# A two-layer decoder trunk: both attention mixers built alike, K, V and Q of a head group projected between attention steps, score matmuls of two heads on two row halves in float32r

## The chip, the cores and the metric

One core of a Trainium2 chip runs the whole program. The engines are TensorE (PE, with its weight loads PEld), VectorE (DVE), ScalarE (ACT), GpSimd (POOL) and SyncE (SP), which here only issues DMAs. The metric is the device time of one execution in microseconds (us); a kernel is given by the median of its runs.

## The reference

The input x is 256 tokens of 1024 float32 values. All weights are float32. In short:

```python
for layer in range(2):
    h = h + 0.5 * swiglu(rmsnorm(h, ffn1_norm[layer]), w_gate, w_up, w_down)   # 1024 -> 2816 -> 1024
    hn = rmsnorm(h, mix_norm[layer])
    if layer == 0:
        h = h + mixer_a(hn, a_w_qkv, a_w_o, pos)        # q, k, v from hn
    else:
        h = h + mixer_b(hn, b_w_q, b_w_o, *shared, pos)  # q from hn, k and v shared
    h = h + 0.5 * swiglu(rmsnorm(h, ffn2_norm[layer]), ...)
    if layer == 0:
        shared = shared_kv(h, kv_norm, kv_w, pos)        # k, v from rmsnorm(h, kv_norm)
return rmsnorm(h, final_norm)
```

There are 16 heads of 64 dimensions; the first 16 of q and k are rotated. Mixer A mixes three dilated causal windows by their softmax denominators, which for 256 tokens equals one softmax in which a key counts as often as it stands in the three windows. Mixer B's blocks are 256 long, so it is causal attention over 256 tokens.

## The kernel before

**Arithmetic.** Every large product is done in float32r with two parts: `parts_of` and `pieces_of` make hi (ACT, rounded to float32r) and lo = value - hi (DVE). A product is hi.hi + hi.lo + lo.hi. Weights come by SP's DMA queue in units of up to 1 MB (`unit`, four raw buffers), are split into `wh` and `wl` tiles of 128 x 1024 (eight buffers each), and go to PE.

**Layout.** The stream hT is kept with features on partitions (8 blocks of 128 x 256 tokens). In the FFN the weights are the stationary operand: a step `product_t` for one block of 128 outputs runs eight matmuls of 512 columns (L193: wh against hi and lo of x side by side) and then eight of 256 (L195: wl against hi). `ffn_blocks` does gate and then up for each of 22 blocks of the hidden layer, with `close` (join, norm row, silu, product; the product with the norm row for up is on POOL, L328) between. `down_t` holds the weights of two output blocks, 22 k-blocks each, and runs one output after the other in runs of 8, 8 and 6.

**Mixers.** In the projections the tokens are stationary and weights move (`product`, L183, L185, L187). Mixer A projects q and k of four heads together (512 columns) and v (256), turns q and k by rotation and transposes, and attends to one group while the next is projected (`weave` takes steps from both by declared costs). The K/V stage between the layers projects all of K and V for mixer B into constants kTb and vb; mixer B then projects q alone, in two halves.

**Attention** (`attend`). For a head: scores in plain float32, 64 rows of PE (L491: one matmul of 128 columns for the first 128 queries, one of 256 for the second), mask, scale and row minimum in one DVE operation (L493), exp with a row sum on ACT (L496), reciprocal on DVE (L498), p times it on ACT (L500), three transposes on PE (L511), split into hi and lo (L92, L94), and four matmuls with v (L528 to L531), of 512, 256, 2 x 128 and 2 x 128 columns. Scores are issued three heads ahead (AHEAD) of the transposes, the values one head behind (LATE). The output projection is `out_t` (L419 to L421).

**Buffers and order.** [...] A scheduler orders each engine's instructions from the order of the source and the buffers that come free; each engine then runs its own list in that order.

Of the kernel before, what the change touches and what calls it, by code (L numbers as in the profile page):

```python
# [28 lines left out]
AHEAD = 3  # L29
LATE = 1  # L30
EXTRA = 1
HURRY = 0.5
FILL_B = 10.0
# [33 lines left out]
def trunk(ctx: ExitStack, tc: tile.TileContext, a: dict, out: bass.AP):  # L67
# [121 lines left out]
    def product_t(ac, ws, xs, first, last):  # L189


        for i, ((wh, wl), x) in enumerate(zip(ws, xs)):
            nc.tensor.matmul(ac, wh, flat(x), start=first and i == 0, stop=False)  # L193
        for i, ((wh, wl), x) in enumerate(zip(ws, xs)):
            nc.tensor.matmul(ac[:, :S], wl, x[:, 0, :], start=False, stop=last and i == len(ws) - 1)  # L195


    def gain(k, gi, name):
        x = xp.tile([P, 2, S], F32R, tag=f"x{k}", name=f"x_{name}_{k}")
        g = gT[:, gi * KD + k:gi * KD + k + 1]  # L200
        parts_of(x[:, 0, :], x[:, 1, :], hT[:, k, :], g)
        return x

    class Norm:
# [41 lines left out]
        def xs(self):  # L246

            return [[tuple(x[:, i, t * P:(t + 1) * P] for i in range(2)) for x in self.x] for t in range(NT)]
# [39 lines left out]
    def down_t(name, w, blocks, norm):  # L288

        for p in range(KD // 2):  # L290
            ws = []
            for k0 in range(0, KF, KD):
                k = min(KD, KF - k0)
                ws += unit(f"{name}_{p}_{k0}", k, S, [(None, rows(w, k0, k, p * S, S))])
            for b in range(2):
                d = 2 * p + b
                ac = acc(f"dn_{name}_{d}")
                cut = [tuple(w[:, b * P:(b + 1) * P] for w in pair) for pair in ws]
                for k0 in range(0, KF, KD):
                    k1 = min(k0 + KD, KF)  # L300
                    product_t(ac, cut[k0:k1], blocks[k0:k1], k0 == 0, k1 == KF)
# [11 lines left out]
    def ffn_blocks(name, wg, wu, norm, first=None):  # L313
# [3 lines left out]
        def times(n, f, w):  # L317
            ac = acc(f"{name}_{n}{f}")
            cols = slice(f % 2 * P, (f % 2 + 1) * P)
            product_t(ac, [(wh[:, cols], wl[:, cols]) for wh, wl in w], norm.x, True, True)  # L320
            return ac
# [21 lines left out]
        for f in range(0, KF, 2):  # L343
# [5 lines left out]
            if f == 0:  # L349
                acs = [[acc(f"{name}_{n}{i}") for n in "gu"] for i in range(2)]  # L350
                for k, pair in enumerate(ws):
                    for i in range(2):
                        for ac, (wh, wl) in zip(acs[i], pair):
                            cols = slice(i * P, (i + 1) * P)
                            product_t(ac, [(wh[:, cols], wl[:, cols])], norm.x[k:k + 1], k == 0, k == KD - 1)
# [9 lines left out]
            wg2, wu2 = zip(*ws)  # L365
# [7 lines left out]
    def ffn(name, layer, which, norm, after, first=None):  # L373
        wg, wu, wd = (a[f"ffn{which}_w_{n}"][layer] for n in ("gate", "up", "down"))
        blocks = ffn_blocks(name, wg, wu, norm, first)
# [5 lines left out]
    def down_last(name, w, nk, blocks, h, weight, part, after, tail=4):  # L381
# [17 lines left out]
        for t in range(NT):  # L399
            for i, (c, o, n) in enumerate(segs[t]):  # L400
                for k, ws in held:
                    product(accs[t][i:i + 1], *blocks[t][k], cols(t, ws)[i:i + 1], False, k == nk - 1)
                hc = h[t][:, c, o:o + n]
# [41 lines left out]
    def rotate(v, t, name):  # L445
# [4 lines left out]
        ta = sp.tile([P, n, ROT], F32, tag="rota", name=f"ra_{name}")  # L450
        tb = sp.tile([P, n, ROT], F32, tag="rotb", name=f"rb_{name}")
# [5 lines left out]
    def turned(src, t, r, name):  # L457

        s = atile([P, 8, DH], name=f"rt_{name}")
        nc.scalar.activation(s.rearrange("p a b -> p (a b)"), src, AF.Copy, scale=r)  # L460
        rotate(s, t, name)
        return s.rearrange("p a b -> p (a b)")

    def transposed(s, dsts, t, name):

        n = s.shape[1] // P
        tr = trt(f"qt_{name}")
        for k in range(n):
            nc.tensor.transpose(tr[:, k * P:(k + 1) * P], s[:, k * P:(k + 1) * P], ident)
        for i, dst in enumerate(dsts):  # L470
            nc.vector.tensor_copy(dst[:, :, t, :],
                                  tr[:, 2 * i * P:(2 * i + 2) * P].rearrange("p (k n) -> p k n", n=P))

    def attend(groups, operands, mask, name, blocks):
# [3 lines left out]
        heads = [(g, j) for g in groups for j in range(HG)]  # L478
        sms = {}

        def scores(g, j):
            qT, kT, _ = operands(g)
            b, p0 = j // 2, (j % 2) * DH
            kh = kT[p0:p0 + DH, b].rearrange("p t n -> p (t n)")
            ps = trt(f"s_{name}{g}_{j}")
            sm = sms[g, j] = atile([P, 3 * P], name=f"sm_{name}{g}_{j}")
            nm = sp.tile([P, NT], F32, tag="nm", name=f"nm_{name}{g}_{j}")
            ls = sp.tile([P, NT], F32, tag="ls", name=f"ls_{name}{g}_{j}")
            segs = [slice(t * P, t * P + (t + 1) * P) for t in range(NT)]
            for t, seg in enumerate(segs):  # L490
                nc.tensor.matmul(ps[:, seg], qT[p0:p0 + DH, b, t, :], kh[:, :(t + 1) * P], start=True, stop=True)  # L491
            for t, seg in enumerate(segs):
                nc.vector.tensor_tensor_reduce(sm[:, seg], ps[:, seg], mask[:, seg], scale=-SCALE, scalar=3e38,  # L493
                                               op0=ALU.add, op1=ALU.min, accum_out=nm[:, t:t + 1])
            for t, seg in enumerate(segs):
                nc.scalar.activation(sm[:, seg], sm[:, seg], AF.Exp, bias=nm[:, t:t + 1], scale=-1.0,  # L496
                                     accum_out=ls[:, t:t + 1])
            nc.vector.reciprocal(ls, ls)  # L498
            for t, seg in enumerate(segs):
                nc.scalar.activation(sm[:, seg], sm[:, seg], AF.Copy, scale=ls[:, t:t + 1])  # L500

        for i in range(AHEAD):
            scores(*heads[i])
            yield 0.65
        pTs, ss = {}, {}
        for n in range(len(heads) + LATE):
            if n < len(heads):
                g, j = heads[n]
                tr = trt(f"pt_{name}{g}_{j}")[:, :3 * P]
                for i in range(3):  # L510
                    nc.tensor.transpose(tr[:, i * P:(i + 1) * P], sms[g, j][:, i * P:(i + 1) * P], ident)  # L511
                pT = pTs[n] = pp.tile([P, 2, 3 * P], F32R, tag="pT", name=f"pT_{name}{g}_{j}")
                parts_of(pT[:, 0], pT[:, 1], tr)
                yield 0.35
            if n + AHEAD < len(heads):
                while operands(heads[n + AHEAD][0]) is None:
                    yield None
                scores(*heads[n + AHEAD])
                yield 0.65
            if n < LATE:  # L520
                continue
            g, j = heads[n - LATE]
            pT = pTs[n - LATE]
            po = acc(f"po_{name}{g}_{j}")
            late = po.rearrange("p (i n) -> p i n", i=2)[:, :, P:]
            pair = slice(j // 2 * P, (j // 2 + 1) * P)
            (h0, l0), (h1, l1) = [[v[:, i, pair] for i in range(2)] for v in operands(g)[2]]
            nc.tensor.matmul(po, h0, pT[:, :, :2 * P], start=True, stop=False)  # L528
            nc.tensor.matmul(po[:, :S], l0, pT[:, 0, :2 * P], start=False, stop=False)
            nc.tensor.matmul(late, h1, pT[:, :, 2 * P:], start=False, stop=False)  # L530
            nc.tensor.matmul(late, l1, pT[:, :, 2 * P:], start=False, stop=True)  # L531
            yield 0.55
            if j % 2 == 0:
                ss[g, j // 2] = etile(f"o_{name}{g}_{j}")
            s = ss[g, j // 2]
            own = slice(j % 2 * DH, (j % 2 + 1) * DH)
            nc.scalar.activation(s[own], po[own, S:], AF.Copy)
            nc.vector.tensor_add(s[own], po[own, :S], s[own])
            if j % 2:
                x = atile([P, 2, S], F32R, name=f"oT_{name}{g}{j // 2}")  # L540
                parts_of(x[:, 0], x[:, 1], s)
                blocks.append(x)
                if len(blocks) == KD:
                    table(AF.Silu, x[:, 0, 0:1].bitcast(F32))

    ATT = HG * 1.55

    def project(ac, pieces, xs, k0):

        for t in range(NT):  # L550
            for k, ps in enumerate(pieces):
                product([ac[t]], *xs[t][k0 + k], [ps], k0 + k == 0, k0 + k == KD - 1)
                yield 3 * ac[t].shape[1] / 2400

    def mixer_a(norm, after):
        xs = norm.xs()
        w, wo = a["a_w_qkv"][0], a["a_w_o"][0]
        blocks = []
        n = HG * DH
        qTs, kTs, vss = {}, {}, {}  # L560
# [200 lines left out]
```

## Time and profile before

| | |
|---|---|
| median of 3 runs | 1017.9 us (1016.5 to 1018.32) |
| profiled execution | 1016.7 us, span 1014.9 us |
| PE busy | 1001.2 us, 99% of the span |
| DVE, ACT, POOL busy | 706.7, 601.8, 150.7 us |
| DMA | 176.03 MB, mean 173 GB/s |
| PE clock granted | 0.999 of full speed |

The page is one execution seen by the profiler; the 1.8 us between its span and its time lie around the program. The stages follow each other on PE with hardly a gap: first FFN to 196 us, mixer A to 322, second FFN to 508, K/V stage to 554, third FFN to 739, mixer B to 819, last FFN to the end. PE's matmuls overlap in a pipeline, so "busy" sums are larger than the time that matmuls take from each other; distances between starts tell that.

### The profile page before, as it was taken

To read this page: it belongs to the slowest core of one execution; us is meant where nothing else is said; L and a number is where in the kernel's file an instruction comes from. 1 tells how busy PE (TensorE), PEld (TensorE's weight loads), DVE (VectorE), ACT (ScalarE), POOL (GpSimd) and SP (SyncE) were. 2 spreads that over 40 slices of the span, in tenths; PEclk is the share of its full clock that TensorE was granted. 3 is DMA by queue.
4 is the path that set the end of the run, shared out by engine and by line. 5 is a ranking of instruction groups with operands and counts; after the bars stand their busy time and mean duration, and the time that the engine had idled before them with its cause. 6 is when DMAs were issued, how large, how long until landed. Compare 5 with 4: busy or idle time off the path is not lost.

```text
span 1014.9 us, 15264 instructions
## 1 busy us (share of the span) xinstructions
PE 1001.2 (99%) x5739; PEld 864.5 (85%) x5739; DVE 706.7 (70%) x1284; ACT 601.8 (59%) x1128; POOL 150.7 (15%) x147
## 2 busy tenths in 40 slices
PE   8999999999999999999999999999999999999997
PEld 6888888888889888888888888888877888888786
DVE  7977765667767777766666777766578777777542
ACT  7756654567776565554555566555459966665531
POOL 3221111100002212211100121210100042112000
PEclk9999999999999999999999999999999999999999
DMA  9875455743334655655475555654552246555511
GB/s 310 260 255 167 160 197 183 228 151 121 126 122 128 205 166 189 195 178 185 171 245 166 191 183 166 193 196 159 200 208 69 84 141 204 168 169 208 187 60 42
DMA packets 152154, 176.03 MB, mean 173 GB/s; under 512 B 3472, under 2 KB 139920, under 8 KB 152080
## 3 DMA queue, kind: packets, MB, share of 16 engines
q1 hardware_dynamic: 151648, 174.50, 52.1%
q8 instruction: 45, 0.74, 0.3%
q10 hardware_dynamic: 432, 0.55, 0.2%
q14 instruction: 29, 0.24, 0.1%
HBM read 173.99 MB, written 1.05 MB: 172 GB/s over the span
## 4 chain that ended last, share of the span: by engine, by line
PE 87%; DVE 5%; POOL 3%; ACT 2%; issue 2%; DMA 0%; POOLq 0%; ACTq 0%; DVEq 0%
PE f_g L193 13%; PE f_u L193 13%; PE dn_f L193 11%; PE f_g L195 7%; PE f_u L195 7%; PE dn_f L195 6%; PE dn_f_d L185 2%; PE dn_f_d L183 2%; PE dn_f_d L187 2%; POOL j_f_u L328 2%; PE qk L183 2%; PE qk L187 1%; PE kv L183 1%; PE qk L185 1%; PE kv L187 1%
## 5 line engine op out<-in xcount | busy, mean ns | idle before, releaser
L193 PE MATMUL f_u<-x_n,wh_f_u 128*128 128x512 f32 x688 | 179.5, 393 | 0.9 <-DVE j_f_g L310 0.9
L193 PE MATMUL f_g<-x_n,wh_f_g 128*128 128x512 f32 x688 | 179.7, 393 | 0.0
L328 POOL TENSOR_TENSOR j_f_u<-j_f_u,r_n 128x256 f32<-128x256 f32 x88 | 98.1, 1116 | 419.7 <-DVE j_f_u L310 358.7
L193 PEld LDWEIGHTS f_u<-x_n,wh_f_u 128*128 128x128 f32 x688 | 124.0, 189 | 23.9 <-DVE j_f_g L310 1.1
L193 PEld LDWEIGHTS f_g<-x_n,wh_f_g 128*128 128x128 f32 x688 | 124.0, 189 | 22.6
L193 PE MATMUL dn_f<-act_f,wh_f 128*128 128x512 f32 x528 | 134.1, 393 | 0.8 <-DVE act_f L94 0.7
L92 ACT ACTIVATE act_f<-j_f_g 128x256 fp32r<-128x256 f32 x88 | 36.7, 418 | 129.2 <-DVE j_f_g L329 129.0
L155 DVE TENSOR_TENSOR wl_f_g<-raw_f_g,wh_f_g 128x1024 fp32r<-128x1024 f32 x86 | 106.4, 1240 | 5.7 <-ACT wh_f_g L154 5.6
L193 PEld LDWEIGHTS dn_f<-act_f,wh_f 128*128 128x128 f32 x528 | 94.6, 189 | 18.4 <-DVE act_f L94 2.0
L155 DVE TENSOR_TENSOR wl_f_u<-raw_f_u,wh_f_u 128x1024 fp32r<-128x1024 f32 x86 | 105.1, 1223 | 7.3 <-ACT wh_f_u L154 7.3
L195 PE MATMUL f_g<-x_n,wl_f_g 128*128 128x256 f32 x688 | 102.9, 282 | 0.0
L195 PE MATMUL f_u<-x_n,wl_f_u 128*128 128x256 f32 x688 | 102.7, 282 | 0.0
L195 PEld LDWEIGHTS f_u<-x_n,wl_f_u 128*128 128x128 f32 x688 | 96.4, 190 | 6.7 <-DVE wl_f_u L155 0.4
L195 PEld LDWEIGHTS f_g<-x_n,wl_f_g 128*128 128x128 f32 x688 | 96.4, 190 | 6.3
L154 ACT ACTIVATE wh_f_g<-raw_f_g 128x1024 fp32r<-128x1024 f32 x86 | 89.5, 1048 | 9.8 <-PE f_g L193 3.8
L225 POOL TENSOR_TENSOR ss_n<-ss_n,sq_n 128x256 f32<-128x256 f32 x42 | 41.6, 991 | 361.0 <-issue 185.1
L154 ACT ACTIVATE wh_f<-raw_f 128x1024 fp32r<-128x1024 f32 x72 | 68.6, 981 | 42.0 <-issue 24.1
L154 ACT ACTIVATE wh_f_u<-raw_f_u 128x1024 fp32r<-128x1024 f32 x86 | 86.8, 1049 | 8.4 <-PE f_g L193 6.5
L155 DVE TENSOR_TENSOR wl_f<-raw_f,wh_f 128x1024 fp32r<-128x1024 f32 x72 | 79.9, 1130 | 16.3 <-PE dn_f L195 13.4
L329 DVE TENSOR_TENSOR j_f_g<-j_f_g,j_f_u 128x256 f32<-128x256 f32 x88 | 37.5, 429 | 61.3 <-POOL j_f_u L328 60.0
L195 PEld LDWEIGHTS dn_f<-act_f,wl_f 128*128 128x128 f32 x528 | 72.8, 190 | 5.6
L195 PE MATMUL dn_f<-act_f,wl_f 128*128 128x256 f32 x528 | 74.6, 282 | 0.0
(197 smaller groups left out, 1739.1 us busy)
## 6 DMA issues: line engine op xcount, KB each, us to landing
raw_f_g<-in_ffn_w_gate_dram SPq DMA_DIRECT2D x43, 1024.0 KB, 5.2
raw_f_u<-in_ffn_w_up_dram SPq DMA_DIRECT2D x43, 1024.0 KB, 5.2
raw_f<-in_ffn_w_down_dram SPq DMA_DIRECT2D x24, 1024.0 KB, 5.2
raw_f_d<-in_ffn_w_down_dram SPq DMA_DIRECT2D x11, 1024.0 KB, 4.9
raw_f<-in_ffn_w_down_dram SPq DMA_DIRECT2D x12, 768.0 KB, 4.5
raw_qk<-in_a_w_qkv_dram SPq DMA_DIRECT2D x16, 512.0 KB, 5.5
raw_kv<-in_kv_w_dram SPq DMA_DIRECT2D x8, 1024.0 KB, 6.2
raw_v<-in_a_w_qkv_dram SPq DMA_DIRECT2D x4, 1024.0 KB, 5.2
```

The source lines that it names most:

```text
L92: nc.scalar.activation(hi, src, AF.Copy, scale=scale)
L154: nc.scalar.activation(wh, r, AF.Copy)
L155: nc.vector.tensor_sub(wl, r, wh.bitcast(F32))
L183: nc.tensor.matmul(ac, xh, wh, start=first, stop=False)
L185: nc.tensor.matmul(ac, xh, wl, start=False, stop=False)
L187: nc.tensor.matmul(ac, xl, wh, start=False, stop=last)
L193: nc.tensor.matmul(ac, wh, flat(x), start=first and i == 0, stop=False)
L195: nc.tensor.matmul(ac[:, :S], wl, x[:, 0, :], start=False, stop=last and i == len(ws) - 1)
L225: nc.gpsimd.tensor_tensor(self.ss, self.ss, sq, op=ALU.add)
L328: nc.gpsimd.tensor_tensor(u, u, norm.row, op=ALU.mult)
L329: nc.vector.tensor_mul(g, g, u)
```

## The change

- **One mixer function for both layers.** `mixer` takes two normed streams (for K and V, and for Q) and is called twice. For each group of four heads it projects k and v together (512 columns), then q (256 columns). All projections of a group but the first 50 steps are woven between attention steps. For mixer B the K/V stream is a second set of x tiles (`kx`), made from hT beside the third FFN; the K/V stage, kTb and vb are gone.
- **Scores by pairs of heads in float32r.** q and k are split into hi and lo (`qk` tiles), and the scores of two heads, which lie on partitions 0-63 and 64-127, are issued alternately: hi.hi, hi.lo, lo.hi for each head and each half of the queries, 12 matmuls for a pair, six of 128 columns and six of 256. Scores run one pair ahead of the transposes.
- **p scaled on GpSimd**, 64 operations `tensor_scalar` in place of 64 on ACT.
- **Values**: v is kept as hi and lo side by side (128 stationary columns for one head), and moves p's hi and lo as 256, 256, 128 and 128 columns; the two halves of the result are added.
- **FFN runs of 16**: gate and up of a block together, 16 matmuls of 512 columns and then 16 of 256; in the down stage two outputs together, 16, 16 and 12, reading the weights unit by unit. Joining comes after both.

The three constants AHEAD, LATE, HURRY and the like go; START = 50 comes. Core of the diff:

```diff
-    def product_t(ac, ws, xs, first, last):
+    def products_t(acs, wss, xs, first, last):
+        for ac, ws in zip(acs, wss):
+            for i, ((wh, wl), x) in enumerate(zip(ws, xs)):
+                nc.tensor.matmul(ac, wh, flat(x), start=first and i == 0, stop=False)
+        for ac, ws in zip(acs, wss):
+            for i, ((wh, wl), x) in enumerate(zip(ws, xs)):
+                nc.tensor.matmul(ac[:, :S], wl, x[:, 0, :], start=False, stop=last and i == len(ws) - 1)
...
     def down_t(name, w, blocks, norm):
         for p in range(KD // 2):
+            acs = [acc(f"dn_{name}_{2 * p + b}") for b in range(2)]
             for k0 in range(0, KF, KD):
                 k = min(KD, KF - k0)
+                ws = unit(f"{name}_{p}_{k0}", k, S, [(None, rows(w, k0, k, p * S, S))])
+                cut = [[tuple(v[:, b * P:(b + 1) * P] for v in pair) for pair in ws] for b in range(2)]
+                products_t(acs, cut, blocks[k0:k0 + k], k0 == 0, k0 + k == KF)
...
             for i in (f, f + 1):
-                gate = times("g", i, wg2)
+                acs = both(i, pair)
                 close_all()
-                done.append((i, gate, times("u", i, wu2)))
+                done.append((i, *acs))
...
+        def scores(p):
+            g, b = divmod(p, HG // 2)
+            (hi, lo), _ = operands(g)
+            ps = [trt(f"s_{name}{p}_{i}") for i in range(2)]
+            for t, seg in enumerate(segs):
+                for n, (q, k) in enumerate(((hi, hi), (hi, lo), (lo, hi))):
+                    for i, own in enumerate(owns):
+                        nc.tensor.matmul(ps[i][:, seg], q[own, b, t, :],
+                                         k[own, 2 + b].rearrange("p t n -> p (t n)")[:, :(t + 1) * P],
+                                         start=n == 0, stop=n == 2)
...
+            nc.vector.reciprocal(flat(ls), flat(ls))
+            for i in range(2):
+                for t, seg in enumerate(segs):
+                    nc.gpsimd.tensor_scalar(sms[p, i][:, seg], sms[p, i][:, seg], ls[:, i, t:t + 1], None, op0=ALU.mult)
...
+        def values(p, pTs):
...
+                for n in range(2):
+                    nc.tensor.matmul(ac, v0, pT[:, n, :S], start=n == 0, stop=False)
+                for n in range(2):
+                    nc.tensor.matmul(ac[:, P:], v1, pT[:, n, S:], start=False, stop=n == 1)
+                nc.scalar.activation(s[own], ac[DH:], AF.Copy)
+                nc.vector.tensor_add(s[own], ac[:DH], s[own])
...
+        for p in range(-1, H // 2):
+            if p + 1 < H // 2:
...
+                scores(p + 1)
+                yield 0.8
+            if p < 0:
                 continue
+            pTs = []
+            for i in range(2):
+                pTs.append(turn(p, i))
+                yield (0.35, 0.5)[i]
+            values(p, pTs)
+            yield 0.9
...
+        def feed():
+            yield from projections(0)
+            for g in range(1, NG):
+                yield from finished(g - 1, projections(g))
+            yield from finished(NG - 1, some(wsteps, 16))
+
+        steps = feed()
+        run(some(steps, START))
+        weave(attend(operands, mask, name, blocks), 20.4, steps, 59.0)
         run(some(wsteps, 4 * EXTRA))
         run(wsteps)
...
-    mixer_a(n1, n2)
+    mixer("a", n1, xs, (w, H * DH), (w, 2 * H * DH), n1, xs, (w, 0), a["a_w_o"][0], masks[:, 0, :], n2)
     ffn("f20", 0, 2, n2, n3)
-    shared_kv(n3)
-    n3.x = [gain(k, 4, "n4") for k in range(KD)]
-    ffn("f11", 1, 1, n3, n5)
-    mixer_b(n5, n6)
+    kx = []
+    ffn("f11", 1, 1, n3, n5, beside=[lambda k=k: kx.append(gain(k, 3, "kx", "kx")) for k in range(KD)])
+    w = a["kv_w"]
+    mixer("b", n3, by_token(kx), (w, 0), (w, H * DH), n5, n5.xs(), (a["b_w_q"][0], 0), a["b_w_o"][0], masks[:, 1, :], n6)
```

More of the change, by code (lines that the diff above doesn't have):

```diff
@@ L202, in gain, with by_token @@
         return x
+    def by_token(xs):
+        return [[tuple(x[:, i, t * P:(t + 1) * P] for i in range(2)) for x in xs] for t in range(NT)]
     class Norm:
@@ L537, in attend @@
[L537 to L553, printed above, removed]
@@ new lines, in finished @@
+        def finished(g, steps):
+            for i, cost in enumerate(steps):
+                yield cost
+                if i == 4:
+                    turn_in(g, 1)
+                    yield 0.45
+                if i == 8:
+                    ready.add(g)
+        wsteps = out_t(f"{name}o", wo, blocks, after)
+        def feed():
[3 more added lines that the diff above has]
+            yield from finished(NG - 1, some(wsteps, 16))
```

302 lines of the change are left out of this document (99 added, 203 removed).

## The prediction

> **What bounds the kernel now.** I read the head of the page, the chain by engine, then the waits of TensorE (PE).
>
> ```profile
> span 1014.9 us, 15264 instructions
> PE 1001.2 (99%) x5739; PEld 864.5 (85%) x5739; DVE 706.7 (70%) x1284; ACT 601.8 (59%) x1128; POOL 150.7 (15%) x147
> PE 87%; DVE 5%; POOL 3%; ACT 2%; issue 2%; DMA 0%; POOLq 0%; ACTq 0%; DVEq 0%
> ...
> PE dn_f L193 <- DVE act_f L94: 0.7, 1, 0.7
> ...
> PE ot_bo L420 <- DVE oT_b L94: 0.6, 1, 0.6
> ...
> PE ot_bo L419 <- ACT oT_b L92: 0.3, 1, 0.3
> PE po_b L528 <- DVE o_b L538: 0.2, 1, 0.2
> ```
>
> PE works in 99% of the span, the chain is 87% PE, and in both mixers together PE waits 1.1 us (last three rows). So the time is PE's stream of matmuls: matmul time taken out is gained, a wait put into it is lost. The "busy" of one matmul is its latency, so I price by distances between starts, from timelines.
>
> ```profile
> 195.96:321.74 125.78, 125.78 (x791) 107.02 (x790) 87.94 (x224) 88.25 (x200) 4.90 (x6) 1.00 0.43 142
> 507.52:553.50 45.98, 45.98 (x214) 38.06 (x213) 29.93 (x53) 24.51 (x32) 2.52 (x2) 1.00 0.62 207
> 738.67:818.73 80.06, 78.92 (x486) 64.83 (x485) 60.19 (x179) 64.24 (x173) 2.53 (x2) 1.00 0.38 131
> ...
> 516.44 0.39 PE L185 MATMUL kv<-wl_kv,x_n 128*128 128x512 f32 x1
> 519.84 0.39 PE L185 MATMUL kv<-wl_kv,x_n 128*128 128x512 f32 x1
> 312.01 0.28 PE L419 MATMUL ot_ao<-oT_a,wh_ao 128*128 128x256 f32 x1
> 318.38 0.28 PE L421 MATMUL ot_ao<-oT_a,wl_ao 128*128 128x256 f32 x1
> 571.01 1.84 PE f_g L193 x8
> 668.78 1.84 PE f_u L193 x8
> ```
>
> The windows (length, then busy time of PE, PEld, DVE, ACT, POOL, then clock, DMA share, GB/s) are mixer A, the K/V stage and mixer B: 125.8 + 46.0 + 80.1 = 251.8 us that the change rebuilds. A matmul of 512 columns costs 3.40 / 15 = 0.227 us (15 starts between the two kv rows), one of 256 columns 6.37 / 53 = 0.120. An FFN step of eight of each costs 97.77 / 35 = 2.793, against 8 x 0.227 + 8 x 0.120 = 2.774: each change between the kinds and back costs 0.02.
>
> **Part 1, scores.**
>
> ```profile
> 755.54 0.40 PE L187 MATMUL bq<-wh_bq,x_n 128*128 128x512 f32 x1
> 755.86 0.93 PE L491 MATMUL s_b<-kTb,bqT 64*128 64x128 f32 x8
> 756.73 0.50 PE L183 MATMUL bq<-wh_bq,x_n 128*128 128x512 f32 x1
> ...
> 768.94 0.39 PE L185 MATMUL bq<-wl_bq,x_n 128*128 128x512 f32 x1
> 769.17 0.40 PE L187 MATMUL bq<-wh_bq,x_n 128*128 128x512 f32 x1
> 769.50 0.92 PE L491 MATMUL s_b<-kTb,bqT 64*128 64x128 f32 x4
> 770.35 0.50 PE L528 MATMUL po_b<-pT_b,bv 128*128 128x512 f32 x1
> 770.69 0.28 PE L529 MATMUL po_b<-pT_b,bv 128*128 128x256 f32 x1
> 770.80 0.28 PE L530 MATMUL po_b<-pT_b,bv 128*128 128x256 f32 x1
> 770.92 0.28 PE L531 MATMUL po_b<-pT_b,bv 128*128 128x256 f32 x1
> 771.04 0.40 PE L183 MATMUL bq<-wh_bq,x_n 128*128 128x512 f32 x1
> ...
> 769.50 0.29 PEld L491 LDWEIGHTS s_b<-kTb,bqT 64*128 64x128 f32 x2 [0.37 <-DVE wl_bo L155]
> 769.50 0.41 PEld L491 LDWEIGHTS s_b<-kTb,bqT 64*128 64x128 f32 x3 [0.37 <-DVE wl_bo L155]
> ```
>
> One head is four float32 passes (x4, two per matmul), 769.50 to 770.35 = 0.85 us; the matmul before it lasts 0.33 and the one behind it 0.34 where 0.23 is usual. Weight loads in the set come 0.41 - 0.29 = 0.12 apart, so a pass of 128 columns is about 0.11 and one of 256 about 0.215 (the float32 rate), 0.65 in all. The rest, 0.10 + 0.20 + 0.11 = 0.41 us, is paid for each visit to the 64-row mode. The x8 row decides this part: two heads, in rows 0-63 and 64-127, took 755.86 to 756.73 = 0.87 us together. The halves overlap fully, weight loads included.
>
> Before: 32 heads x 0.65, less one shared pair (0.65), and 32 visits x 0.41: 33.3 us. After: per pair 12 float32r matmuls that alternate between the halves. With 256 columns one is 0.12. With 128 columns no row shows one; its bounds are 0.06 (half of 0.12) and 0.215 (two float32 passes of 0.11 each, rounded down). I take 0.11, the pace of the weight loads. A pair is 3 x 0.11 + 3 x 0.12 = 0.69. In the changed kernel's instruction order the eight sets of a mixer stand in ten stretches (pairs 5 and 7 are cut in two, and six matmuls of pair 7 stand in unmixed threes: +0.33). Sum: 16 x 0.69 + 20 x 0.41 + 0.7 = 19.9. **Gain 13.4 us.** If float32r halves did not overlap, 16 x 0.69 = 11.0 of it is lost; at 0.215 per 128 columns 16 x 3 x 0.105 = 5.0; at 0.06 there are 2.4 more.
>
> [...]
>
> **Part 2, values.** A head is now 0.23 + 3 x 0.12 = 0.59 us (L528 to L531), then two matmuls of 256 columns and two of 128: 2 x 0.12 + 2 x 0.11 = 0.46. **Gain 32 x 0.13 = 4.1 us.** Per 128-column matmul at 0.06 it is 3.2 more; at 0.215 it is 6.7 less, a loss of 2.6.
>
> **Part 3, projections.** Mixer B's q becomes 192 matmuls of 256 columns (23.0) for 96 of 512 (21.8): **loss 1.2 us**. All others keep their columns: the K/V stage is not saved but moves into mixer B, with its 8 MB of DMA (DMA was 0.62 busy there and is 0.38 in mixer B, so no bound). Transposes keep their number. The p scalings leave ACT; the hi/lo split of q and k comes to ACT and DVE, where copies go. DVE's 87.9 + 29.9 + 60.2 = 178 us stay about that in some 240, so DVE does not become the bound.
>
> **Part 4, FFN.** 80 gate/up steps and 36 down steps merge 8 + 8 into 16 + 16 and spare one change each: **gain 116 x 0.02 = 2.3 us**. The down stage reads its last activation after some 11 us where it was half that, so the 0.7 us behind act_f go: **gain 0.7**. The last two outputs of a down stage now end 0.7 us apart, not 7.7; the next stage reads their x after more than 5 us of other matmuls, which covers two lots of some 2 us on DVE and ACT. I cost that, and gate and up joining together, at nothing; without the cover it is about 2 us at the end of each of three such stages.
>
> **Part 5, new waits.** Before, scores ran three heads ahead; now one pair. The chain from a pair's last score to its first transpose:
>
> ```profile
> L493 DVE CUSTOM_DVE_ANT_0 sm_a<-s_a,masks 128x256 f32<-128x256 f32 x16 | 6.7, 417 | 0.0
> L493 DVE CUSTOM_DVE_ANT_0 sm_a<-s_a,masks 128x128 f32<-128x128 f32 x16 | 4.6, 291 | 10.0 <-PE s_a L491 9.8
> L496 ACT ACTIVATE sm_a<-sm_a,nm_a 128x256 f32<-128x256 f32 x16 | 7.9, 494 | 0.0
> L498 DVE RECIPROCAL ls_a<-ls_a 128x2 f32<-128x2 f32 x16 | 2.6, 162 | 5.2 <-ACT sm_a L496 5.2
> L94 DVE TENSOR_TENSOR pT_a<-pt_a,pT_a 128x384 fp32r<-128x384 f32 x16 | 8.8, 553 | 2.0 <-ACT pT_a L92 2.0
> L722 POOL TENSOR_SCALAR var<-ssq,ssq 128x1 f32<-128x1 f32 x2 | 0.6, 299 | 58.5 <-ACT sq L713 58.5
> ...
> 41.41 1.59 POOL L328 TENSOR_TENSOR j_f_u<-j_f_u,r_n 128x256 f32<-128x256 f32 x1 [4.04 <-DVE j_f_u L310]
> ...
> 53.00 0.73 POOL L328 TENSOR_TENSOR j_f_u<-j_f_u,r_n 128x256 f32<-128x256 f32 x1 [4.21 <-DVE j_f_u L310]
> ...
> 41.19 1.21 DVE L155 TENSOR_TENSOR wl_f_u<-raw_f_u,wh_f_u 128x1024 fp32r<-128x1024 f32 x1
> ```
>
> Four reductions 2 x (0.29 + 0.42) = 1.4, a last exponential 0.5, a reciprocal 0.16, two scalings on POOL, and an estimated 0.1 for each of some eight hand-overs (no row isolates one). A one-input scaling on POOL stands in no row: for 256 columns it lies between 0.30 (a single column) and 0.73 (two inputs, undisturbed); I take 0.45, and 0.35 for 128. Sum 3.7.
>
> In the new order pair 0 has 18 q matmuls, the next scores and three more q behind it: 21 x 0.12 + 0.69 + 0.41 = 3.6, a wait of about 0.2. Pairs 1 to 5 have some 6 to 18 us. Pairs 5, 6 and 7 crowd at the end. Behind pair 6 stand 6 transposes, 5 output matmuls, 4 of values and pair 7's scores in two stretches: 0.7 + 0.6 + 0.5 + 1.8 = 3.6, against 3.7 and 0.55 to 1 for pair 5's parts in the same queues: wait about 0.9. Pair 7's reciprocal stands in DVE's queue behind pair 5's two adds, its own reductions, parts of pairs 5 and 6 and a weight split of 1.21: added up (an estimate), its transposes can start 11 us after pair 6's scores, and PE comes to them after 9.2: wait about 1.8. With 0.3 at the last output and 1.1 for the three score buffers, which transposes share, a mixer waits 0.2 + 0.9 + 1.8 + 0.3 + 1.1 = 4.3 us, both 8.6, against 1.1 now: **loss 7.5 us**. Bounds: nothing (the order as good as today's) and 16 (rival 2).
>
> **Sum.** -13.4 - 4.1 + 1.2 - 2.3 - 0.7 + 7.5 = -11.8. The profiled execution took 1016.7 us (span 1014.9 and 1.8 around it), 1.2 below the median of 1017.9; 1016.7 - 11.8 = 1004.9, about 1006 as a median.
>
> **Rivals.** 1, *the scores do not do what they say*: float32r halves take turns. For it: no row shows float32r in a half. Against: the float32 row of 0.87. Then -11.8 + 11.0: about 1017.
>
> 2, *slower, by the scaling on POOL*. Place: POOL's four scalings per pair, behind which pair p's transposes and, in DVE's queue, the next pair's parts wait. The trace shows the mechanism: POOL's multiplication that met a DVE split (41.19 to 42.40) ended at 43.00 and took 1.59, the one beside an idle DVE took 0.73. At 1.59 or nearly for each, two scalings cost some 2.8 in place of 0.8: 2 us more at pairs 0 and 6, and 4 at pair 7, where both pairs' scalings add up: 8 a mixer, 16 in all, about 1022. It decides from 6 us a mixer on. Against: most pairs have 6 us and more in hand, and few splits stand in the crowded end.
>
> [...]
>
> 3, *128 columns of float32r cost 0.215*. For it: the kernel before pairs columns up to 256 for its values. Against: weight loads 0.12 apart. Then -11.8 + 5.0 + 6.7 (the 4.1 gained becomes 2.6 lost): about 1018.
>
> 4, *few new waits*: 1 us a mixer, about 999.
>
> **How the numbers follow.** The forecast has a chance of 0.64 and, with waits of 2 to 7 us a mixer and 128 columns between 0.06 and 0.13, a range of 1000 to 1011. Rival 1 has 0.07, rival 2 0.13, rival 3 0.09, rival 4 0.07. The range of 999 to 1018 takes in rivals 1 and 3 at their centres and leaves out rival 2 and the outer halves of the others. A measurement of this kernel can tell about 0.2%, 2 us, from no change. Faster by that: forecast, rival 4 and a part of rivals 1 and 3 that falls short, 0.76; same: most of rivals 1 and 3, 0.10; slower: rival 2 and the rest, 0.14.
>
> **What would show it.** After: visits of score sets at about 1.1 us for 12 matmuls (1.8 would be rival 1); p scalings at 0.3 to 0.5 us (1.2 and more is rival 2); 128-column values 0.11 apart (rival 3); runs x16 in the FFN; mixers of some 118 to 121 us each, and PE waits of pt on POOL and po on DVE of 3 to 5 us a mixer. Mixers over 124 us, or PE waits over 9 us in one, make the prediction wrong.

## The result and the profile after

The changed kernel takes 1022.9 us (median, 1020.6 to 1027.4), the kernel before 1017.9 (1016.4 to 1018.3): a ratio of 1.0058, 95% interval 1.0037 to 1.0078. It is slower by 0.6%, where 1.2% faster was forecast. The executions of the kernel before lie in two groups about 1.6 us apart, and its profiled one, 1016.7 us, is of the faster group. The profiled execution of the changed kernel took 1023.3 us. The head of its page and its chain by engine:

```profile
span 1021.5 us, 15730 instructions
...
PE 994.7 (97%) x5899; PEld 871.0 (85%) x5899; DVE 724.6 (71%) x1252; ACT 592.0 (58%) x1092; POOL 178.1 (17%) x211
...
PE 88%; ACT 6%; DVE 3%; POOL 1%; issue 1%; DMA 0%; POOLq 0%; ACTq 0%; DVEq 0%
```

PE's busy time is 6.5 us shorter and the span is 6.6 us longer: PE fell from 99% to 97% of it, and ACT has 6% of the chain where it had 2%. What PE waited for (us in total, times, longest):

```profile
PE pt_a L494 <- POOL sm_a L489: 3.7, 5, 1.2
PE pt_b L494 <- POOL sm_b L489: 3.6, 5, 1.2
PE f_u L191 <- DVE j_f_g L309: 2.3, 4, 0.9
PE po_a L508 <- ACT pT_a L89: 2.2, 1, 2.2
PE po_a L508 <- DVE o_a L512: 1.2, 2, 0.8
```

The names end in a and b for mixers A and B; f_u belongs to the FFN. Both mixers wait alike: transposes for p scaled on GpSimd, values for the copies of their own transposes on ACT and DVE. The stretches of time show where it went. The first and last window are mixers A and B; the others are 3.41 us long and follow each other in pairs. Columns: length, busy time of PE, PEld, DVE, ACT, POOL, then granted clock, DMA share, GB/s.

```profile
194.55:325.72 131.17, 123.15 (x822) 107.65 (x821) 87.22 (x208) 81.69 (x183) 30.97 (x38) 0.97 0.40 128
228.61:232.02 3.41, 1.75 (x16) 1.22 (x13) 2.21 (x15) 2.98 (x14) 1.95 (x3) 1.00 0.85 308
232.02:235.43 3.41, 3.41 (x15) 3.13 (x15) 0.73 (x2) 0.68 (x3) 3.41 (x6) 0.50 0.00 0
307.11:310.53 3.42, 1.43 (x10) 0.80 (x9) 2.11 (x3) 1.92 (x4) 3.35 (x4) 1.00 0.00 0
310.53:313.94 3.41, 3.41 (x18) 3.41 (x18) 1.82 (x4) 1.18 (x3) 0.66 (x1) 0.50 0.82 269
696.89:827.75 130.86, 122.74 (x822) 107.49 (x821) 87.29 (x208) 81.78 (x183) 29.99 (x38) 0.97 0.40 128
```

The mixers take 131.2 + 130.9 = 262.0 us, where mixer A, the K/V stage and mixer B took 251.8. PE idles 8.0 and 8.1 us in them. And twice in each mixer the clock is 0.50 for 3.41 us, right behind a stretch in which PE was busy for only 1.75 or 1.43 us in mixer A, and 1.91 or 1.65 in mixer B. The first of these in PE's timeline:

```profile
229.40 0.28 PE L184 MATMUL q_a<-wh_qa,x_n 128*128 128x256 f32 x1
230.75 0.33 PE L494 MATMUL pt_a<-ident,sm_a 128*128 128x128 f32 x1 [1.08 <-POOL sm_a L489]
231.67 0.44 PE L494 MATMUL pt_a<-ident,sm_a 128*128 128x128 f32 x2 [0.58 <-POOL sm_a L489]
...
233.16 0.42 PE L180 MATMUL q_a<-wh_qa,x_n 128*128 128x256 f32 x1
233.37 0.42 PE L182 MATMUL q_a<-wl_qa,x_n 128*128 128x256 f32 x1
...
235.60 0.28 PE L180 MATMUL q_a<-wh_qa,x_n 128*128 128x256 f32 x1
235.72 0.28 PE L182 MATMUL q_a<-wl_qa,x_n 128*128 128x256 f32 x1
```

Pair 0's transposes wait twice; after that a matmul of 256 columns takes 0.21 us from start to start, until at 235.43 it is 0.12 again. Idle time in the row of PE is not all that a wait costs.

From the distances between PE's starts (as in the prediction), mixer A's 131.2 us are, by estimate: 117.9 of matmuls at their usual distances, 9.9 by which the starts that waited stand further apart (8.0 of it idle time; the rest fits that a matmul of 256 columns is busy for 0.28 us, while the next usually starts after 0.12), and 3.4 for half of the two stretches at half clock. Mixer B has 117.6, 10.0 and 3.2. The prediction had 117.2 (251.8 less the old waits of 1.1 and less 13.4 and 4.1, plus 1.2, halved), 4.3, and nothing.

### The profile page after: what moved, and what is told of

Its sections match the earlier page's. It is cut to its first block, busy times and chain, and to the rows that moved or that the text cites. A ratio compares the mean times of both kernels' runs of the same rounds, so it can differ in the third digit from the quotient of the medians.

```text
span 1021.5 us, 15730 instructions
## 1 busy us (share of the span) xinstructions
PE 994.7 (97%) x5899; PEld 871.0 (85%) x5899; DVE 724.6 (71%) x1252; ACT 592.0 (58%) x1092; POOL 178.1 (17%) x211
## 4 chain that ended last, share of the span: by engine, by line
PE 88%; ACT 6%; DVE 3%; POOL 1%; issue 1%; DMA 0%; POOLq 0%; ACTq 0%; DVEq 0%
PE f_u L191 16%; PE f_g L191 15%; PE dn_f L191 12%; PE f_u L194 8%; PE f_g L194 8%; PE dn_f L194 6%; PE dn_f_d L182 2%; PE dn_f_d L180 2%; PE dn_f_d L184 2%; PE kv_b L184 1%; PE kv_b L182 1%; PE kv_b L180 1%; PE kv_a L184 1%; PE kv_a L180 1%; PE kv_a L182 1%
## 5 line engine op out<-in xcount | busy, mean ns | idle before, releaser
L191 PEld LDWEIGHTS f_u<-x_n,wh_f_u 128*128 128x128 f32 x688 | 128.8, 188 | 30.2 <-issue 2.1
L327 POOL TENSOR_TENSOR j_f_u<-j_f_u,r_n 128x256 f32<-128x256 f32 x88 | 76.0, 865 | 383.0 <-DVE j_f_u L309 363.8
L191 PE MATMUL dn_f<-act_f,wh_f 128*128 128x512 f32 x528 | 126.5, 391 | 0.0
L152 DVE TENSOR_TENSOR wl_f_u<-raw_f_u,wh_f_u 128x1024 fp32r<-128x1024 f32 x86 | 119.6, 1392 | 1.8 <-ACT wh_f_u L151 1.7
L191 PEld LDWEIGHTS dn_f<-act_f,wh_f 128*128 128x128 f32 x528 | 96.8, 188 | 18.6
L194 PEld LDWEIGHTS f_u<-x_n,wl_f_u 128*128 128x128 f32 x688 | 91.7, 192 | 0.5 <-DVE wl_f_u L152 0.4
L325 ACT ACTIVATE j_f_g<-j_f_g 128x256 f32<-128x256 f32 x88 | 36.8, 418 | 63.2 <-DVE j_f_g L324 62.7
L194 PEld LDWEIGHTS dn_f<-act_f,wl_f 128*128 128x128 f32 x528 | 68.1, 191 | 2.8
L194 PE MATMUL dn_f<-act_f,wl_f 128*128 128x256 f32 x528 | 69.0, 283 | 0.0
```

Of the source, the lines that this page charges most:

```text
L152: nc.vector.tensor_sub(wl, r, wh.bitcast(F32))
L325: nc.scalar.activation(g, g, AF.Silu)
L327: nc.gpsimd.tensor_tensor(u, u, norm.row, op=ALU.mult)
```

## Experiments

The table has all kernels but one (the stalls, below). Idle is the length of the mixer's window less PE's busy time, for mixers A and B; the last column counts stretches of 3.41 us at half clock in both.

| kernel | median us | ratio to before | idle A, B | half clock |
|---|---|---|---|---|
| changed kernel | 1022.9 | 1.0058 (1.0037 to 1.0078) | 8.0, 8.1 | 4 |
| scaling on ACT | 1020.2 | 1.0027 (1.0017 to 1.0037) | 7.2, 7.4 | 2 |
| scaling on DVE | 1017.4 | 0.9991 (0.9983 to 1.0000) | 6.2, 5.9 | 2 |
| filled waits | 1018.1 | 1.0005 (0.9996 to 1.0013) | 5.6, 5.7 | 0 |
| FFN part alone | 1014.1 | 0.9961 (0.9948 to 0.9973) | 0.4, 1.6 (kernel before: 0.0, 1.1) | 0 |
| late values | 1014.4 | 0.9971 (0.9961 to 0.9982) | 3.9, 4.1 | 2 |
| late values, DVE | 1012.2 | 0.9944 (0.9931 to 0.9958) | 2.8, 2.9 | 0 |
| DVE, respread | 1012.5 | 0.9946 (0.9933 to 0.9958) | 3.8, 3.8 | 1 |
| late values, DVE, respread | 1014.9 | 0.9971 (0.9960 to 0.9983) | 3.4, 3.5 | 0 |
| late values, DVE, START 46 | 1012.1 | 0.9943 (0.9927 to 0.9960) | 3.2, 3.3 | 0 |
| late values, DVE and GpSimd | 1011.4 | 0.9936 (0.9921 to 0.9951) | 2.8, 2.9 | 0 |
| the same, scores in one tile | 1016.8 | 0.9998 (0.9989 to 1.0007) | 5.2, 5.1 | 3 |

**Scaling on ACT.**

```diff
-  nc.gpsimd.tensor_scalar(sms[p, i][:, seg], sms[p, i][:, seg], ls[:, i, t:t + 1], None, op0=ALU.mult)
+  nc.scalar.activation(sms[p, i][:, seg], sms[p, i][:, seg], AF.Copy, scale=ls[:, i, t:t + 1])
```

> The changed kernel with the 64 scalings of p on ACT (activation Copy with a scale, as the kernel before did) in place of GpSimd; nothing else. Theory: the miss comes from waits of TensorE in the attention (9.9 us a mixer in place of 4.3) and from the four stretches of 3.4 us at half clock behind them (6.8 us of work lost in all); both come to a good part from the scaling on GpSimd, which took 0.60 and 0.92 us where 0.35 and 0.45 were taken. A scaling on ACT took 0.40 and 0.50 in the kernel before. Then the waits fall by 2 to 3 us a mixer, at least two of the four half-clock stretches go, and the time is 1010 to 1016. Rival A: the waits come from scores that run only one pair ahead and from the order of ACT's queue; ACT, with 1.4 us more for each pair, hands over p's transposes later, and the time is 1021 to 1028.

Measured 1020.2: 2.7 us less, which is hardly clear of the noise and short of the theory's 1016. PE's waits for transposes fell from 3.7 to 0.9 us a mixer, but one wait of values grew:

```profile
PE po_a L508 <- ACT pT_a L89: 3.7, 1, 3.7
...
PE pt_a L494 <- ACT sm_a L489: 0.9, 2, 0.7
```

ACT's timeline in this kernel, ahead of that wait's end at 259.3, tells why:

```profile
256.69 1.48 ACT L489 ACTIVATE sm_a<-sm_a,ls_a 128x128 f32<-128x128 f32 x4
258.07 0.46 ACT L567 ACTIVATE rt_a<-kv_a,c_n 128x256 f32<-128x256 f32 x1
258.43 0.46 ACT L89 ACTIVATE vs_a<-kv_a,c_n 128x256 fp32r<-128x256 f32 x1
258.79 0.86 ACT L89 ACTIVATE pT_a<-pt_a 128x384 fp32r<-128x384 f32 x2
```

The copy of pair 2's transposes (the last row) stands behind pair 3's exps and scalings and the copies of k and v. The scalings put 1.48 us more in front of it, and the wait went from 2.2 to 3.7. So there are two causes side by side: scaled p that comes late, and ACT's order.

**Scaling on DVE.**

```diff
-  nc.gpsimd.tensor_scalar(sms[p, i][:, seg], sms[p, i][:, seg], ls[:, i, t:t + 1], None, op0=ALU.mult)
+  nc.vector.tensor_scalar_mul(sms[p, i][:, seg], sms[p, i][:, seg], ls[:, i, t:t + 1])
```

> The changed kernel with the 64 scalings of p on DVE (tensor_scalar_mul) in place of GpSimd; nothing else. A one-input DVE operation of 128 columns took 0.28 us (diag), so an estimate of 0.28 and 0.42 for the two forms, 1.3 us a pair where GpSimd took 3.0. Theory (scaling on GpSimd behind most waits and half-clock stretches): the shortest chain of the three, time 1009 to 1015. Rival A (one pair ahead and ACT's order behind the waits): within 2 us of the changed kernel, 1021 to 1025, since DVE has the room (87 of 131 us busy) and gives nothing back.

Measured 1017.4, between the two expectations. A scaling took 0.28 and 0.35 us on DVE, against 0.60 to 0.92 on GpSimd. The waits of transposes went to 0.6 a mixer, that of values for ACT stayed at 2.2:

```profile
PE po_a L508 <- ACT pT_a L89: 2.2, 1, 2.2
...
PE pt_a L494 <- DVE sm_a L489: 0.6, 1, 0.6
```

**Filled waits.**

```diff
+            for _ in range(FILL.get((p, i), (0, 0))[0]):
+                nc.tensor.matmul(bank, fill[:, :P], fill, start=True, stop=True)
             for n in range(3):
+                if n == 1:
+                    for _ in range(FILL.get((p, i), (0, 0))[1]):
+                        nc.tensor.matmul(bank[:, 3 * P:], fill[:, :P], fill[:, :P], start=True, stop=True)
                 nc.tensor.transpose(tr[:, n * P:(n + 1) * P], sms[p, i][:, n * P:(n + 1) * P], ident)
```

> The changed kernel with 23 bfloat16 matmuls of no use in each mixer, written to the free bank ahead of and between p's transposes of pair 0 and pair 7, where the changed kernel's TensorE waits for GpSimd (4 of 512 columns and 7 of 128 at pair 0, 5 and 7 at pair 7); the scaling stays on GpSimd. The scheduler also moves some q matmuls ahead of pair 0's transposes. Theory: the half clock follows stretches in which TensorE does little; with the filling, the four half-clock stretches go, and the time falls by some 5 to 7 us to 1016 to 1019, the fillers taking no more than the waits did. Rival B: the half clock has nothing to do with these waits, the stretches stay at two a mixer, and the fillers (1.3 us at pair 0 and 1.5 at pair 7) leave the time at 1022 to 1026.

Measured 1018.1, as the theory had it: 4.8 us less with 23 useless matmuls more in each mixer, and the four stretches at half clock are gone. The scheduler's shift of q matmuls at pair 0 helped too, so this run alone does not price the clock.

**Stalls in the kernel before.**

```diff
+STALL = {4: 2, 8: 3, 12: 4, 16: 5}
...
             for i in (f, f + 1):
+                for _ in range(STALL.get(i, 0) if name != "f10" else 0):
+                    nc.gpsimd.tensor_scalar(norm.x[0][:, 0], norm.x[0][:, 0].bitcast(F32), 1.0, None, op0=ALU.mult)
                 gate = times("g", i, wg2)
```

> The kernel before, with twelve stalls of TensorE put into its second, third and fourth FFN: ahead of blocks 4, 8, 12 and 16 the first x tile is multiplied by 1.0 in place on GpSimd, 2, 3, 4 and 5 times, and the next matmuls need it. At 0.92 us each (the time of 256 columns in the changed kernel), less some 0.8 us of matmuls that do not need the tile, TensorE waits about 1.0, 2.0, 2.9 and 3.8 us. Theory: a stretch at half clock follows where TensorE had been idle for about half of a 3.4 us stretch; so none behind the waits of 1.0, some behind 2.0, all behind 2.9 and 3.8; each costs 1.7 us more than its wait. With the waits (29 us) and 6 to 9 stretches the time is 1057 to 1063. Rival B (no half clock from waits): 1047, and the clock stays at full speed.

Measured 1088.7, 1.070 times before (1.067 to 1.072). The waits were longer than expected, 51.0 us in all, since a multiplication took 1.39 us on average where 0.92 was expected. The profiled execution took 1090.8 us, 74.1 more than that of the kernel before; the rest, 74.1 - 51.0 = 23.1 us, stands beside ten places at half clock. Eight of these lasted two stretches, 6.83 us, so that there were 18 stretches where 6 to 9 were expected. Three waits and what followed each (windows as above):

```profile
604.65:606.22 1.57, 0.00 (x1) 0.00 (x0) 1.57 (x3) 0.93 (x3) 1.44 (x2) 1.00 0.00 0
606.22:609.63 3.41, 3.41 (x19) 2.95 (x20) 2.78 (x4) 0.46 (x2) 1.65 (x1) 1.00 0.83 255
895.78:898.42 2.64, 0.00 (x1) 0.00 (x1) 2.64 (x5) 2.64 (x5) 2.50 (x2) 1.00 0.00 0
898.42:901.83 3.41, 3.41 (x19) 2.98 (x20) 2.78 (x4) 0.49 (x2) 1.64 (x1) 1.00 0.89 266
345.46:347.89 2.43, 0.00 (x1) 0.00 (x0) 2.43 (x5) 2.43 (x4) 2.34 (x2) 1.00 0.00 0
347.89:351.30 3.41, 3.19 (x8) 2.51 (x9) 2.79 (x4) 0.45 (x2) 1.81 (x2) 0.50 0.79 254
```

A wait of 1.57 us cost only itself. Of two waits of 2.6 us one was followed by the half clock and the other not (the one from 345.46 lasted until 348.11; its window ends where the clock changes). All nine of 3.9 us and more were. So waits of 3.9 us and more brought the half clock by themselves, in a kernel without any of the change's attention.

**Late values.**

```diff
-        for p in range(-1, H // 2):
+        pTs = {}
+        for p in range(-1, H // 2 + 1):
             if p + 1 < H // 2:
...
                 scores(p + 1)
                 yield 0.8
-            if p < 0:
-                continue
-            pTs = []
-            for i in range(2):
-                pTs.append(turn(p, i))
-                yield (0.35, 0.5)[i]
-            values(p, pTs)
-            yield 0.9
+            if p > 0:
+                values(p - 1, pTs.pop(p - 1))
+                yield 0.9
+            if 0 <= p < H // 2:
+                pTs[p] = []
+                for i in range(2):
+                    pTs[p].append(turn(p, i))
+                    yield (0.35, 0.5)[i]
```

> The changed kernel with one thing altered: the value matmuls of a pair come one step later, behind the next pair's scores, and not right behind their own transposes; the scaling stays on GpSimd. Theory C (after the first runs): two kinds of wait stand beside each other. One is transposes that wait for the scaled p (5.4 us a mixer in the changed kernel), the other values that wait for the copies of their transposes through ACT and DVE (2.2 us in one place at pair 2, 1.2 more at pair 3 and 6). Taking the second kind away gives 3 us a mixer: 1016 to 1019. Rival: with the values gone from between, the next pair's transposes come sooner and wait for GpSimd by as much more: 1021 to 1025.

Measured 1014.4: 8.5 us less, with GpSimd still scaling. This one change of order turns the loss into a gain of 0.3%. Mixer A and the remaining waits for GpSimd, all at pair 0:

```profile
194.55:321.71 127.16, 123.27 (x823) 107.37 (x821) 85.57 (x207) 81.61 (x180) 32.02 (x37) 0.99 0.41 132
```

```profile
PE pt_a L494 <- POOL sm_a L489: 1.7, 2, 1.1
```

More than the theory said went away: the next pair's transposes also wait less, and two of the four half-clock stretches are gone.

**Late values with the scaling on DVE.** Both edits.

> The kernel with the scaling on DVE (1017.4 us), and besides the value matmuls one step later, behind the next pair's scores. Theory C: its waits of 2.2, 1.1 and 0.3 us of values for ACT and DVE in each mixer go and its one half-clock stretch a mixer as well (1.7): 4 to 5 us a mixer less, 1008 to 1011. Rival: the waits of values come back as waits of transposes for the scaled p: 1015 to 1018.

Measured 1012.2. No half clock, idle 2.8 us:

```profile
194.44:320.12 125.68, 122.90 (x822) 106.90 (x821) 92.48 (x238) 81.04 (x179) 4.39 (x5) 1.00 0.41 133
```

It misses the 1008 to 1011 because the matmuls themselves took more: about 121 us a mixer without waits and half clock, for about 118 with the scaling on DVE alone (estimates from the distances between starts). The timeline shows one place:

```profile
247.94 0.32 PE L473 MATMUL s_a<-qkh_a 64*128 64x128 f32 x1
...
248.82 0.50 PE L180 MATMUL kv_a<-wh_kva,x_n 128*128 128x512 f32 x1
```

Six score matmuls of one head alone, 247.94 to 248.82 = 0.88 us, as long as twelve of two heads that alternate. In this order the scheduler cuts three pairs of eight in this way, with other matmuls between the two heads.

**The end of the mixers.**

```diff
-            yield from finished(NG - 1, some(wsteps, 16))
+            yield from finished(NG - 1, some(wsteps, 20))
...
-        weave(attend(operands, mask, name, blocks), 20.4, steps, 59.0)
-        run(some(wsteps, 4 * EXTRA))
+        weave(attend(operands, mask, name, blocks), 20.4, steps, 55.0)
```

> The kernel with the scaling on DVE (1017.4 us), and besides the output projection spread further: 20 of its steps between the attention steps in place of 16 and none straight behind, and the declared total of the woven steps 55 in place of 59, so that they last to the end. It tells whether the end of a mixer (pairs 6 and 7 crowded) is what costs. By theory C little: its waits there sum to about 1 us a mixer, so 1015 to 1017. Rival D (the crowded end behind most of the loss): 1010 to 1013.

> Both of the two alterations on the kernel with the scaling on DVE: values one step later, and the output projection spread over 20 steps with a total of 55. Theory C: as with the late values alone, 1007 to 1011. Rival D: lower than that by 3 us or more.

The first gave 1012.5, 4.9 us less than the scaling on DVE alone and inside the range of rival D. But the wait of 2.2 us at pair 2, far from the end, went as well: the spreading shifts every step. With the late values it made things worse, 1014.9 for 1012.2, which neither expectation had. The order of the steps is worth several us either way, and I did not find a rule for it.

**Two smaller tries on the late kernel**: an earlier start of the attention, and the first head's scalings on DVE, the second's on GpSimd.

```diff
-START = 50
+START = 46
```

```diff
-  nc.vector.tensor_scalar_mul(sms[p, i][:, seg], sms[p, i][:, seg], ls[:, i, t:t + 1])
+  eng = (nc.vector, nc.gpsimd)[i]
+  eng.tensor_scalar(sms[p, i][:, seg], sms[p, i][:, seg], ls[:, i, t:t + 1], None, op0=ALU.mult)
```

> The kernel with the scaling on DVE and late values (1012.2 us), with 46 steps of projection ahead of the attention in place of 50. If the crowded end still costs, 1009 to 1011; if pair 0 then waits longer for its operands and scaled p, 1013 to 1015.

> The kernel with late values, with the scaling of a pair's first head on DVE and of its second on GpSimd, side by side. The second head's transposes come later anyway, so that GpSimd's 1.5 us for it are covered, and DVE has 0.65 us less a pair: 1010 to 1013, against 1012.2 with DVE alone and 1014.4 with GpSimd alone. If GpSimd's second half still holds up the transposes, 1013 to 1015.

1012.1 is no difference. 1011.4 is the fastest kernel here, 0.64% below the kernel before; against DVE alone the intervals overlap.

**Both heads' scores in one tile of two banks**, on the last kernel; `scp` is a pool of its own, and `trp` held the three buffers that scores, transposes and small sums shared.

```diff
-  trp = ctx.enter_context(tc.tile_pool(name="trp", bufs=3, space=PS))
+  trp = ctx.enter_context(tc.tile_pool(name="trp", bufs=1, space=PS))
+  scp = ctx.enter_context(tc.tile_pool(name="scp", bufs=1, space=PS))
...
-  ps = [trt(f"s_{name}{p}_{i}") for i in range(2)]
+  both = scp.tile([P, 2, 512], F32, tag="sc", name=f"s_{name}{p}")
+  ps = [both[:, i] for i in range(2)]
```

> The kernel with late values and the scaling split between DVE and GpSimd (1011.4 us), with both heads' scores of a pair in one tile of two PSUM banks and the third bank alone for transposes. With late values the traces show that in three of eight pairs a mixer the six matmuls of one head went before the six of the other, each six in 0.88 us where a whole pair of twelve took 0.88: in one tile the heads alternate. If that is what the stream of matmuls lost beside its waits (121 us a mixer against 117.6 in the changed kernel), 2 to 3 us a mixer come back: 1006 to 1009. Rival: the transposes, now with one bank, wait for their copies, and the time is 1012 to 1016.

Both halves of the expectation came true, and the rival decided it: 1016.8 lies even above its 1012 to 1016. Five of eight pairs stand whole, the other three are cut into parts in most of which both heads still alternate, and the matmuls without waits and half clock came down to about 118 or 119 us a mixer; but transposes waited for their copies, and there were three stretches at half clock:

```profile
PE pt_a L497 <- DVE pT_a L92: 3.5, 4, 1.2
```

**The FFN part alone**, on the kernel before: `products_t`, `down_t` and `ffn_blocks` as in the change shown above, its core being

```diff
-  product_t(ac, [(wh[:, cols], wl[:, cols]) for wh, wl in w], norm.x, True, True)
+  products_t(acs, [[(wh[:, cols], wl[:, cols]) for wh, wl in w] for w in pair], norm.x, True, True)
```

> The kernel before with the change's FFN part alone: gate and up in runs of 16, down stages of two outputs at a time in runs of 16, 16 and 12. The prediction gave 2.3 + 0.7 = 3.0 us less, 1014.9 as a median. What the two traces show in the FFN stages: gate and up stages 0.7 us longer in sum (a wait of the next up matmuls for DVE at the second block of a stage, 0.6 each), down stages 2.2 shorter: 1.5 us less, 1016.4. A rival, that the last two outputs of a down stage ending together costs the next stage its cover: 1018 to 1020.

Measured 1014.1, 4.1 us less by the medians; between the profiled executions, 1016.7 and 1014.1, it is 2.6, and the stages of the two traces add up to that. The down stages gave 2.3 (62.49, 61.84 and 61.68 us became 61.25 each, to 0.01). Another 2.3 came from a place that neither the prediction nor the expectation named. The first two rows are from the waits of the kernel before, the third from this one's:

```profile
PE h L702 <- ACT vb L703: 2.2, 1, 2.2
PE col_n L230 <- POOL ss_n L225: 0.4, 1, 0.4
PE col_n L232 <- POOL ss_n L227: 1.7, 4, 0.4
```

The transposes of h behind the last gate and up stage waited for ACT, and with runs of 16 they do not. The gate and up stages stayed as they were in sum. But the three stages that follow a down stage (mixer A, the K/V stage and mixer B) became 0.6 us longer each, 1.9 in all; most of it is the new waits of col_n, a matmul of the norm, for GpSimd. So the rival's lost cover is real, though smaller than it had it.

## Why the prediction was wrong

**Part 1, right.** One visit of the changed kernel, with the matmuls around it:

```profile
252.51 0.39 PE L184 MATMUL kv_a<-wh_kva,x_n 128*128 128x512 f32 x1
252.83 0.33 PE L473 MATMUL s_a<-qkh_a 64*128 64x128 f32 x2
...
253.71 0.39 PE L180 MATMUL q_a<-wh_qa,x_n 128*128 128x256 f32 x1
253.94 0.28 PE L182 MATMUL q_a<-wl_qa,x_n 128*128 128x256 f32 x1
```

Twelve matmuls in 0.88 us (252.83 to 253.71), 0.09 more before and 0.11 behind: 1.08 for the forecast 1.10. Float32r halves overlap, so rival 1 is out, as long as the heads alternate.

**Parts 2 and 3, right in kind.** A head's values (L508, L510):

```profile
250.79 0.51 PE L508 MATMUL po_a<-pT_a,vs_a 128*128 128x256 f32 x2
251.13 0.33 PE L510 MATMUL po_a<-pT_a,vs_a 128*128 128x128 f32 x2
251.30 0.45 PE L180 MATMUL kv_a<-wh_kva,x_n 128*128 128x512 f32 x1
```

They took 0.51 us for the forecast 0.46; 128 columns took 0.085 each, so rival 3 is out. A q matmul took 0.12. Together the stream came to 117.9 and 117.6 us for 117.2: the arithmetic of parts 1 to 3 held.

**Part 4, the sum nearly right, its places partly wrong.** Alone, it gained 2.6 us between profiled executions for the forecast 3.0. "I cost that, and gate and up joining together, at nothing" failed three ways. The stages behind the down stages lost 1.9 us of their cover. In the changed kernel joining made the next up matmuls wait for DVE (three new waits of about 0.45 us, which took back most of the 1.6 us that the 80 changes were to spare). And it took away the 2.2 us at h. That these nearly cancel is luck. In the changed kernel the stages outside the mixers are 3.7 us shorter.

**Part 5 failed.** It had 4.3 us of waits a mixer; 9.9 came, and the mixers took 131 us, above the 124 that the prediction named as a sign of being wrong. Its terms: 0.2 at pair 0 was 1.7 of idle time, for the most part since a scaling on GpSimd took this (mean ns of one behind the busy time; with the scaling on DVE 0.6 was left):

```profile
L489 POOL TENSOR_SCALAR sm_a<-sm_a,ls_a 128x256 f32<-128x256 f32 x16 | 14.9, 933 | 0.0
L489 POOL TENSOR_SCALAR sm_a<-sm_a,ls_a 128x128 f32<-128x128 f32 x16 | 10.8, 675 | 82.9 <-DVE ls_a L486 55.9 <-DVE nm_a L481 26.9
```

I had taken 0.45 and 0.35, the lower part of the bounds of 0.30 and 0.73; 0.92 lies above them both. The 0.1 for each hand-over was my estimate, and no run shows it as one figure: at pair 0 of mixer A an engine started 0.04 (ACT behind DVE), 0.03 (DVE behind ACT), 0.18 (GpSimd behind DVE) and 0.05 us (PE behind GpSimd) after the one before it had ended. Pair 7 waited 2.0 us for the forecast 1.8. The 0.9 at pair 6 and the 1.1 for the score buffers did not come: no transpose of pair 6 and no score matmul of mixer A waited. "Pairs 1 to 5 have some 6 to 18 us" looked at transposes alone: the values behind them waited 2.2 us for ACT at pair 2 and 1.2 for DVE in two places further on, which the prediction did not cost at all but for 0.3 at the end. In idle time this is the larger mistake, 3.4 us a mixer against some 1.7 at pairs 0 and 7. Moving the values gave 8.5 us and a quicker scaling 5.5; but the move also cut the waits for GpSimd from 3.7 to 1.7 us a mixer, so it does not price the waits of the values alone.

**The clock was missing altogether.** 3.4 and 3.2 us a mixer, 6.6 in all, came as half clock behind stretches with waits; the longest wait of the kernel before in its trace, 2.2 us at h, brought none (the clock was 1.00 in the 3.41 us behind it). In sum: 5.6 and 5.7 for waits, 6.6 for the clock, 1.1 for the stream, less 0.7 in the FFN stages, is 18.3 of the 18.4 us between the 1004.9 forecast for a profiled execution and 1023.3.

**Rival 2** named this time, about 1022, and the scaling on GpSimd, but not why; that its number came out is luck. It wanted 1.59 us for nearly each scaling beside a DVE split. Only two of 64, at pair 7, met one so that they took 1.63 in place of 0.60; two more took 1.08 in place of 0.92. So what the prediction read from 1.59 against 0.73 us came where the two met, and stretched one scaling of each mixer by 1.0 us. With GpSimd out of it 5.5 us were gained, not 16.

## What to carry to other kernels

Where TensorE is the bound, cost each new dependence twice: once for the wait, and once for a stretch at half clock that may follow it (here 3.41 us at 0.50, about 1.7 us lost each time). In the changed kernel that came four times behind waits of 1.5 to 2 us close together, but not each time. When a step is issued right behind the one whose result it needs, look at every copy queued ahead of it on the other engines; putting another step's matmuls between the two was worth more here than a faster operation (8.5 us against 5.5). And price an operation that no row shows by something with the same shape on the same engine, or keep the upper bound well above the nearest row.

## What the hardware showed

**The half clock came on a grid, and idle time alone did not bring it.** All starts of half-clock stretches in the changed kernel lie whole multiples of 3.413 us apart (580.27 / 170): 232.02, 310.53, 733.78 and 812.29 are 0, 23, 147 and 170 steps. In the run with stalls, of the two waits of 2.6 us, the first began the half clock after 2.43 us idle in one step; eight steps before the half clock at 924.74 lies 897.43, a border that cut the second into 1.65 and 0.99 us, and it brought none. But how long PE was idle in a step is not the rule. The first two rows are the changed kernel at pair 2, the last two the kernel with the scaling on DVE:

```profile
255.91:259.32 3.41, 1.59 (x14) 1.35 (x13) 1.48 (x9) 3.40 (x13) 0.77 (x2) 1.00 0.88 279
259.32:262.73 3.41, 3.04 (x22) 2.90 (x23) 2.42 (x7) 1.55 (x4) 2.37 (x3) 1.00 0.07 29
297.99:301.40 3.41, 2.97 (x22) 2.30 (x21) 2.53 (x9) 2.14 (x9) 0.00 (x0) 1.00 0.89 302
301.40:304.82 3.42, 3.42 (x18) 3.41 (x17) 1.63 (x7) 2.10 (x4) 0.00 (x0) 0.50 0.02 5
```

At pair 2 PE was busy for 1.59 us, less than the 1.75 that brought the half clock at pair 0, and it brought none. In the kernel with the scaling on DVE the half clock came behind a step in which PE was busy for 2.97 us and idle for 0.44; the respread kernel shows the same. So busy time as the profile counts it does not decide alone. What does is open: at pair 2 PE did six transposes and six full q matmuls, at pair 0 three transposes, four full matmuls and some scores on 64 rows, and in the step from 297.99 for a large part scores on 64 rows. That such scores count for less would fit, but no run here varies them alone. At pair 0 a step half idle was enough (busy for 1.75 of 3.41 us), and in the respread kernel and the one with the scaling on DVE even 0.43 and 0.44 us of idle time were.

**Six score matmuls of one head alone took as long as twelve of two heads that alternate**: 0.88 us each, on 64 rows (247.94 to 248.82 with late values and the scaling on DVE, 252.83 to 253.71 in the changed kernel). So the overlap of the two halves was lost where the order of the instructions parted the heads.
